# The experts' last 32 slots on 512-column tiles, with their first products ahead of the wide ones

## The chip, the cores and the metric

The kernel runs on one core of a Trainium2 chip. The metric is the device time of one execution in microseconds; lower is better. TensorE does the matrix products, VectorE (DVE in the rows) and ScalarE (ACT) move and transform their results, GpSimd (POOL) issues the indirect DMAs, and SyncE (SP) issues the weight loads. Each engine works off its own instructions in a fixed order, and semaphores hold an instruction back until what it needs is there.

## What is computed

One decoder layer on 2048 tokens of width 1024: a mixer (gated linear attention beside dilated attention), then a mixture of 32 experts, then a last norm. The change lies in the experts. Each token goes to two experts; an expert is a SwiGLU block:

```python
def expert_block(args):
    toks, e = args
    xb = x[toks]
    hb = jax.nn.silu(xb @ w1[e]) * (xb @ w3[e])
    return hb @ w2[e]
y = lax.map(expert_block, (row_tok.reshape(n_blk, MOE_BLOCK), blk_exp))
y = y.reshape(R, D).astype(jnp.float32) * row_w[:, None]
out = jnp.zeros((M, D), jnp.float32).at[row_tok].add(y)
```

w1 and w3 are 1024x512 per expert, w2 is 512x1024, all float32.

## The kernel before

An expert has 160 slots for tokens: a first block of 128 and the **last 32**. The loop over the experts (L1439) is unrolled. For each expert:

- **Weights** (L1292): six parts of 1 MB (half of w1, half of w3, the other halves, two halves of w2) are loaded by SP into `raw`, a pool of six buffers, so one expert's worth. ScalarE rounds each part to `hi` (L1308) and VectorE takes the rest, `lo = raw - hi` (L1308); these two share a pool of five pairs. A buffer of `raw` comes free when it has been split and when the last slots have used it too.
- **First block, first products** (`up`, L1347): 48 wide products of 512 columns, three for each of 8 slices of the 1024 rows and each of w1 and w3 (`nh·hi`, `nl·hi`, `nh·lo`; L1358 to L1360). ScalarE's silu (L1372) and VectorE's product (L1373) make `h`.
- **Last slots, first products** (in `up`, L1367): plain float32 products with 32 columns of weights each. The array is used as four tiles of 32 columns, and the four hold the two halves of w1 and the two halves of w3, 256 columns each: 8 slices x 4 tiles = 32 products. The silu (L1378) and product (L1379) make `hr`.
- **Turning the inner values** (`across`, L1382): four transposes of `h` (L1385) and the split into `hh` and `hl` (L1388); two transposes of `hr` (L1393) and the copy `ht` (L1395).
- **The next expert's inputs** (`turn`, L1330): eight transposes of the gathered rows (L1333), split into `nh` and `nl` (L1336). Every fourth expert, `turn_last` does the same for the last slots of four experts (`nr`).
- **Second products** (`down`, L1398): 24 wide products (L1407 to L1409), scaled out of PSUM by both engines (L1411, L1413) and added to `acc` in DRAM by an indirect DMA (L1415); then 16 products of the last slots on four tiles of 256 columns (L1423), scaled to `yr` (L1426) and added by a second DMA of 128 rows of 1 KB (L1427).

From expert 16 on, a finished block of tokens is taken from `acc`, normed and given out beside each expert (`take`, `scale`, `give`).

The order of each engine's instructions is worked out when the kernel is built: of what a timeline model holds to be ready, the piece that stands first in the program goes first, so a later piece can slip in where an earlier one is not ready. `behind` (L125) forces one instruction after another without a semaphore. A plain float32 product appears as two MATMUL records, one for each pass.

Of the kernel before, what the change touches and what calls it, by code (L numbers as in the profile page):

```python
# [60 lines left out]
class Layer:  # L61
# [1123 lines left out]
    def moe(self):  # L1185
        tc, nc, a = self.tc, self.nc, self.a
        with self.moest as st:
# [9 lines left out]
            acc4 = self.acc.rearrange("t (g c) -> (t g) c", g=4)  # L1197
# [3 lines left out]
            i4A = keep.tile([128, NE], I32, name="i4")  # L1201
# [3 lines left out]
            def entries(es):  # L1205
# [10 lines left out]
                f4 = gp.tile([128, NE], F32, name="f4", bufs=1)  # L1216
                nc.vector.tensor_copy(f4[:, es], irA[:, es, 0])
                nc.vector.tensor_scalar(f4[:, es], f4[:, es], 4.0, self.gcol, OP.mult, OP.add)
                nc.vector.tensor_copy(i4A[:, es], f4[:, es])
# [110 lines left out]
            def turn(G):  # L1330
                tp = tps.tile([128, KD, 128], F32, name="tp")
                for k in range(KD):
                    nc.tensor.transpose(tp[:, k, :], G[:, k * 128:(k + 1) * 128], self.ident)  # L1333
# [13 lines left out]
            def up(w, x, nr=None):  # L1347
# [5 lines left out]
                for half in range(2):  # L1353
                    for m in range(2):
                        raw, hi, lo = w[m][half]
                        for kk in range(4):
                            k = half * 4 + kk
                            nc.tensor.matmul(ps[m], nh[:, k, :], hi[:, kk, :], start=k == 0, stop=False)  # L1358
                            nc.tensor.matmul(ps[m], nl[:, k, :], hi[:, kk, :], start=False, stop=False)  # L1359
                            nc.tensor.matmul(ps[m], nh[:, k, :], lo[:, kk, :], start=False, stop=k == KD - 1)  # L1360
                pr = None
                if nr is not None:
                    pr = rps.tile([128, 256], F32, name="r")
                    for k in range(KD):
                        for g in range(4):
                            raw = w[g // 2][k // 4][0]
                            nc.tensor.matmul(pr[32 * g:32 * g + 32], nr[:, k, :], raw[:, k % 4, (g % 2) * 256:(g % 2) * 256 + 256],  # L1367
                                             start=k == 0, stop=k == KD - 1, skip_group_check=True, tile_position=(0, 32 * g))
# [5 lines left out]
                hr = None  # L1374
                if nr is not None:
                    hr = gp.tile([128, 256], F32, name="hr", bufs=1)
                    by, to = (lambda t: t.rearrange("t (p k) -> t k p", k=2)), hr[64:128].rearrange("t (k p) -> t k p", k=2)
                    nc.scalar.activation(to, by(pr[0:64]), AF.Silu)  # L1378
                    nc.vector.tensor_tensor(to, by(pr[64:128]), to, OP.mult)  # L1379
                return h, hr  # L1380

            def across(h, hr):  # L1382
                tp = mm.tile([128, 4, 128], F32, name="mm")
                for k in range(4):
                    nc.tensor.transpose(tp[:, k, :], h[:, k * 128:(k + 1) * 128], self.ident)  # L1385
# [3 lines left out]
                ht = None  # L1389
                if hr is not None:  # L1390
                    tr = rps.tile([128, 2, 64], F32, name="r")
                    for c in range(2):
                        nc.tensor.transpose(tr[:, c, :], hr[64:128, c * 128:(c + 1) * 128], self.ident[64:128, 64:128])  # L1393
                    ht = gp.tile([128, 2, 2, 32], F32, name="ht", bufs=1)
                    nc.vector.tensor_copy(ht, tr.rearrange("p c (u s) -> p u c s", u=2))  # L1395
                return hh, hl, ht

            def down(w2, x, it, irs, e=None):  # L1398
                hh, hl, ht = x
# [17 lines left out]
                if ht is not None:  # L1417
                    ir, i4 = irs
                    pr = rps.tile([128, 256], F32, name="r")
                    for k in range(4):  # L1420
                        raw = w2[k // 2][0]
                        for g in range(4):
                            nc.tensor.matmul(pr[32 * g:32 * g + 32], ht[:, k // 2, k % 2, :], raw[:, k % 2, g * 256:g * 256 + 256],  # L1423
                                             start=k == 0, stop=k == 3, skip_group_check=True, tile_position=(0, 32 * g))
                    yr = yp.tile([128, 256], F32, name="yr", bufs=1)
                    nc.vector.tensor_scalar(yr, pr, ir[:, 1:2].bitcast(F32), None, OP.mult)  # L1426
                    added(nc.gpsimd.indirect_dma_start(out=acc4, out_offset=bass.IndirectOffsetOnAxis(ap=i4, axis=0),  # L1427
                                                       in_=yr, in_offset=None, compute_op=OP.add), e)
# [10 lines left out]
            for e in range(NE):  # L1439
# [9 lines left out]
                h = across(*up((w1, w3), x, nr[:, :, at:at + 32]))  # L1449
                at += 32  # L1450
                if e + 1 < NE:
                    x = turn(G.pop(e + 1))
                    if e % 4 == 1:
                        nr, at = turn_last(R, 32 * min(4, NE - 1 - e)), 0
                    for t, c in zip(self.turned, self.crossed):
                        self.behind(t, c, "what the tensor engine waits for comes first")
                if e == 0:
                    self.firstst.close()
                    yp = pool("e_y", 1)
                down(w2, h, itA[:, e], (irA[:, e], i4A[:, e:e + 1]), e)  # L1460
# [124 lines left out]
```

## Time and profile before

| what | value |
|---|---|
| three runs | 2205.49, 2211.96, 2216.13 us; median 2211.96 |
| the profiled execution | 2214.42 us; its span 2212.6 us |
| TensorE busy | 2096.8 us, 95% of the span |
| VectorE, ScalarE, GpSimd busy | 57%, 48%, 24% of the span |
| mean granted TensorE clock | 0.972 of full speed |
| the experts' stage | from about 1316 us to about 2178 us of the span |

The busy share of TensorE counts a product from its start to its modelled end, and products overlap; idle time and lost time between products is read from the timeline, by the distance from one start to the next.

### The profile page before, as it was taken

The page shows a single profiled execution, that of the slowest core. Times are in us where ns is not written, and L with a number is a line of the kernel's source. Part 1 is how long each engine was busy: PE and PEld are TensorE (multiplying, and loading weights), DVE is VectorE, ACT ScalarE, POOL GpSimd, SP SyncE. Part 2 cuts the span into 40 slices and gives each one's busy share as a digit, 9 for nine tenths or more (in the row PEclk, how much of TensorE's full clock was granted, in tenths as well). Part 3 has the DMA queues.
Part 4 walks back from the last instruction along what each step waited for, and adds up shares of the span by engine and source line. Part 5 has one row for each costly group of instructions (what it writes and reads, how often), then busy time and mean ns, then how long its engine had stood idle before and what let it go on. Part 6 is the DMA issues. An engine that isn't in the chain of part 4 may idle for free.

```text
span 2212.6 us, 38640 instructions
## 1 busy us (share of the span) xinstructions
PE 2096.8 (95%) x15306; PEld 1571.0 (71%) x15306; DVE 1272.2 (57%) x2469; ACT 1057.2 (48%) x1809; POOL 530.6 (24%) x370
## 2 busy tenths in 40 slices
PE   7999999999997999999999968999999999999993
PEld 7799889799885666666667756666767766666662
DVE  5203346424435556666646775676767677766762
ACT  5412335522323367767723334465555556555651
POOL 2000000000002002441421253632222344424432
PEclk9999999999998999999989969999999999999996
DMA  8333333333325614453358827788878889988973
GB/s 252 109 127 102 115 117 117 98 113 124 96 85 179 192 68 134 150 132 92 96 174 283 253 100 249 253 315 300 291 278 301 310 307 351 329 303 294 319 276 106
DMA packets 189033, 436.59 MB, mean 197 GB/s; under 512 B 35041, under 2 KB 106530, under 8 KB 162978
## 3 DMA queue, kind: packets, MB, share of 16 engines
q1 hardware_dynamic: 139090, 347.65, 44.5%
q0 software_dynamic: 21488, 60.36, 10.3%
q10 hardware_dynamic: 28272, 26.09, 4.0%
q8 instruction: 122, 2.00, 0.4%
q14 instruction: 61, 0.50, 0.1%
HBM read 342.48 MB, written 92.08 MB: 196 GB/s over the span
## 4 chain that ended last, share of the span: by engine, by line
PE 83%; DMA 6%; DVE 4%; issue 2%; POOL 2%; ACT 1%; SPq 0%; ACTq 0%; DVEq 0%; POOLq 0%
PE r L1367 5%; PE s L561 5%; PE mm L1360 5%; PE mm L1358 5%; PE mm L1359 4%; PE mm L216 4%; PE mm L217 4%; PE mm L193 4%; PE mm L218 4%; PE mm L194 4%; PE mm L195 4%; PE po L590 4%; PE pt L575 4%; PE mm L1407 3%; PE mm L1408 3%; PE r L1423 3%
## 5 line engine op out<-in xcount | busy, mean ns | idle before, releaser
L1308 DVE TENSOR_TENSOR lo<-raw,hi 128x2048 fp32r<-128x2048 f32 x192 | 438.3, 2290 | 133.0 <-ACT hi L1308 132.3
L1308 ACT CAST hi<-raw 128x2048 fp32r<-128x2048 f32 x192 | 364.6, 1905 | 191.7 <-DMA raw<-expert_w 170.8
L567 ACT ACTIVATE P<-P,st 128x256 f32<-128x256 f32 (+1 forms) x384 | 173.9, 455 | 96.9 <-DVE st L565 92.6
L216 PE MATMUL mm<-whi,nh 128*128 128x256 f32 x768 | 219.9, 286 | 0.0
L218 PE MATMUL mm<-whi,nl 128*128 128x256 f32 x768 | 218.2, 284 | 0.0
L217 PE MATMUL mm<-wlo,nh 128*128 128x256 f32 x768 | 217.8, 284 | 0.0
L1360 PE MATMUL mm<-lo,nh 128*128 128x512 f32 x512 | 206.6, 405 | 1.1 <-DVE lo L1308 1.1
L1358 PE MATMUL mm<-hi,nh 128*128 128x512 f32 x512 | 205.0, 401 | 1.7 <-ACT nh L1336 1.3
L1359 PE MATMUL mm<-hi,nl 128*128 128x512 f32 x512 | 201.6, 394 | 0.0
L131 POOL TENSOR_TENSOR ss<-ss,mhalf 128x1 f32<-128x1 f32 (+1 forms) x32 | 28.9, 902 | 695.2 <-DVE ss L130 695.1
L565 DVE CUSTOM_DVE_ANT_0 P<-s,amask 128x256 f32<-128x256 f32 (+1 forms) x384 | 124.9, 362 | 66.2 <-PE s L561 42.9
L193 PE MATMUL mm<-nh,whi 128*128 128x512 f32 x384 | 154.5, 402 | 0.0
L194 PE MATMUL mm<-nl,whi 128*128 128x512 f32 x384 | 153.1, 399 | 0.0
L195 PE MATMUL mm<-nh,wlo 128*128 128x512 f32 x384 | 152.7, 398 | 0.0
L1367 PE MATMUL r<-raw,nr 128*32 128x256 f32 x2048 | 148.5, 383 | 0.0
L216 PEld LDWEIGHTS mm<-whi,nh 128*128 128x128 f32 x768 | 145.5, 189 | 2.0 <-issue 0.7
L217 PEld LDWEIGHTS mm<-wlo,nh 128*128 128x128 f32 x768 | 145.6, 190 | 0.8 <-DVE wlo L179 0.4
L218 PEld LDWEIGHTS mm<-whi,nl 128*128 128x128 f32 x768 | 144.9, 189 | 0.1
L1415 POOL DMA_INDIRECT acc<-y,it x32 | 84.6, 2642 | 205.6 <-ACT y L1411 195.8
L561 PE MATMUL s<-k,q 64*128 64x256 f32 (+1 forms) x768 | 132.8, 416 | 0.4 <-DVE st L565 0.3
L1360 PEld LDWEIGHTS mm<-lo,nh 128*128 128x128 f32 x512 | 96.6, 189 | 42.7 <-issue 14.0
L179 DVE TENSOR_TENSOR wlo<-raw,whi 128x1024 fp32r<-128x1024 f32 x48 | 57.0, 1220 | 112.7 <-ACT whi L178 112.7
(345 smaller groups left out, 4252.3 us busy)
## 6 DMA issues: line engine op xcount, KB each, us to landing
raw<-expert_w SPq DMA_DIRECT2D x192, 1024.0 KB, 9.7
raw<-w_in ACTq DMA_DIRECT2D x48, 512.0 KB, 5.0
fb<-fac SPq DMA_DIRECT2D x24, 384.0 KB, 7.5
x<-x SPq DMA_DIRECT2D x16, 512.0 KB, 5.0
og<-og SPq DMA_DIRECT2D x32, 256.0 KB, 3.8
xr<-x SPq DMA_DIRECT2D x32, 256.0 KB, 3.2
v<-av SPq DMA_DIRECT2D x8, 1024.0 KB, 7.2
hp<-xr SPq DMA_DIRECT2D x32, 256.0 KB, 2.3
```

Source lines behind the costliest of these rows:

```text
L193: nc.tensor.matmul(ps, hi[:, k, ms], nh[q][:, k, :], start=k == 0, stop=False)
L194: nc.tensor.matmul(ps, hi[:, k, ms], nl[q][:, k, :], start=False, stop=False)
L195: nc.tensor.matmul(ps, lo[:, k, ms], nh[q][:, k, :], start=False, stop=k == KD - 1)
L216: nc.tensor.matmul(ps[:, j, :], h, hi[:, k, :], start=j == 0 and k == 0, stop=False, skip_group_check=True)
L217: nc.tensor.matmul(ps[:, j, :], h, lo[:, k, :], start=False, stop=False, skip_group_check=True)
L218: nc.tensor.matmul(ps[:, j, :], l, hi[:, k, :], start=False, stop=k == KD - 1, skip_group_check=True)
L561: nc.tensor.matmul(ps[:, h, 0:w], KQ[p, br][hs, 128 * blk:128 * blk + 128], keys(br, blk, KQ[p, "k"][hs]), start=True, stop=True, skip_gro ...
L1308: split = nc.scalar.copy(hi, raw), nc.vector.tensor_tensor(lo, raw, hi.bitcast(F32), OP.subtract)
L1358: nc.tensor.matmul(ps[m], nh[:, k, :], hi[:, kk, :], start=k == 0, stop=False)
L1359: nc.tensor.matmul(ps[m], nl[:, k, :], hi[:, kk, :], start=False, stop=False)
L1360: nc.tensor.matmul(ps[m], nh[:, k, :], lo[:, kk, :], start=False, stop=k == KD - 1)
L1367: nc.tensor.matmul(pr[32 * g:32 * g + 32], nr[:, k, :], raw[:, k % 4, (g % 2) * 256:(g % 2) * 256 + 256], start=k == 0, stop=k == KD - 1, ...
```

## The change

The last slots' work is taken out of `up`, `across` and `down` into functions of its own.

- `up_last`: the four tiles now hold w1 and w3 for an even slice and w1 and w3 for an odd slice, 512 columns each: 4 pairs of slices x 4 tiles = 16 products. The even and the odd sums stand in PSUM rows 0 to 63 and 64 to 127; a copy by ScalarE (64x512) and an addition by VectorE (64x512) join them, then silu (32x512) and two products (32x256 each) make `hr`.
- `down_last`: 8 products of 512 columns instead of 16 of 256; again two sums, joined by a scaled copy on ScalarE (64x512) and a scaled addition on VectorE (64x512); the DMA adds 64 rows of 2 KB instead of 128 rows of 1 KB.
- Order: `up_last` stands ahead of `up`, and each half of the wide products is put behind the last slots' products that read the same half. `down_last` stands ahead of the transposes of `h`, which are put behind its last product; the transposes for the next expert are put behind those. The wide second products come last. In expert 0 the wide first products stand first and the next expert's inputs are turned ahead of the transposes of `h`.

```diff
-            def up(w, x, nr=None):
+            def up_last(w, nr):
+                pr = rps.tile([128, 512], F32, name="r")
+                halves = []
+                for k in range(0, KD, 2):
+                    for g in range(4):
+                        kk, raw = k + g // 2, w[g % 2][k // 4][0]
+                        lasts = nc.tensor.matmul(pr[32 * g:32 * g + 32], nr[:, kk, :], raw[:, kk % 4, :],
+                                                 start=k == 0, stop=k == KD - 2, skip_group_check=True, tile_position=(0, 32 * g))
+                    halves.append(lasts)
...
+                nc.scalar.copy(sm, pr[64:128])
+                nc.vector.tensor_tensor(sm, pr[0:64], sm, OP.add)
+                nc.scalar.activation(sg[32:64], sm[0:32], AF.Silu)
+                by = lambda t, u: t[:, 256 * u:256 * u + 256].rearrange("t (p k) -> t k p", k=2)
+                for u in range(2):
+                    to = hr[64 + 32 * u:96 + 32 * u].rearrange("t (k p) -> t k p", k=2)
+                    nc.vector.tensor_tensor(to, by(sm[32:64], u), by(sg[32:64], u), OP.mult)
+                return hr, halves[1::2]
+            def up(w, x, halves=None):
...
+                            first = nc.tensor.matmul(ps[m], nh[:, k, :], hi[:, kk, :], start=k == 0, stop=False)
+                            if halves and kk == 0:
+                                self.behind(first, halves[half], "the raw weights come free early")
...
+                    self.inner = nc.tensor.transpose(tp[:, k, :], h[:, k * 128:(k + 1) * 128], self.ident)
+                    if after is not None:
+                        self.behind(self.inner, after, "the last slots' products cover the inner values")
...
+            def down_last(w2, hr, ir, i2, e):
+                ht = across_last(hr)
+                pr = rps.tile([128, 512], F32, name="r")
+                for k in range(0, 4, 2):
+                    raw = w2[k // 2][0]
+                    for g in range(4):
+                        kk, f = g // 2, g % 2
+                        last = nc.tensor.matmul(pr[32 * g:32 * g + 32], ht[:, k // 2, kk, :], raw[:, kk, f * 512:f * 512 + 512],
+                                                start=k == 0, stop=k == 2, skip_group_check=True, tile_position=(0, 32 * g))
+                yr = yp.tile([64, 512], F32, name="yr", bufs=1)
+                nc.scalar.activation(yr, pr[64:128], AF.Copy, scale=ir[64:128, 1:2].bitcast(F32))
+                nc.vector.scalar_tensor_tensor(yr, pr[0:64], ir[0:64, 1:2].bitcast(F32), yr, op0=OP.mult, op1=OP.add)
+                added(nc.gpsimd.indirect_dma_start(out=acc2, out_offset=bass.IndirectOffsetOnAxis(ap=i2, axis=0),
+                                                   in_=yr, in_offset=None, compute_op=OP.add), e)
+                return last
...
-                h = across(*up((w1, w3), x, nr[:, :, at:at + 32]))
+                if e == 0:
+                    h = up((w1, w3), x)
+                hr, halves = up_last((w1, w3), nr[:, :, at:at + 32])
+                if e:
+                    h = up((w1, w3), x, halves)
                 at += 32
+                if e == 0:
+                    x = turn(G.pop(1))
...
+                h = across(h, down_last(w2, hr, irA[:, e], i2A[:, e:e + 1], e))
                 if e + 1 < NE:
-                    x = turn(G.pop(e + 1))
+                    if e:
+                        x = turn(G.pop(e + 1), self.inner)
...
-                down(w2, h, itA[:, e], (irA[:, e], i4A[:, e:e + 1]), e)
+                down(w2, h, itA[:, e], e)
```

## Rows read from the trace of the kernel before

**Rows 1.** Stretches of the experts' stage: length, busy by engine, PEclk, DMA share, GB/s

```profile
1630.00:1680.00 50.00, 50.00 (x364) 35.20 (x364) 35.80 (x26) 29.16 (x22) 12.14 (x6) 1.00 0.83 298
2030.00:2080.00 50.00, 48.47 (x330) 33.16 (x329) 35.16 (x28) 30.67 (x25) 22.91 (x12) 1.00 0.97 349
```

**Rows 2.** What TensorE waited for, 1330 to 2180: total us, times, longest

```profile
PE mm L1385 <- DVE h L1373: 11.0, 3, 6.9
PE mm L1407 <- ACT hh L1388: 3.4, 4, 1.6
PE r L1393 <- DVE hr L1379: 2.4, 3, 1.1
```

**Rows 3.** What SP's load queue waited for, 1380 to 2180: total us, times, longest

```profile
SPq L1303 <- PE r L1367: 443.4, 58, 19.5
SPq L1303 <- PE r L1423: 209.5, 58, 15.0
```

**Rows 4.** One stretch of 3 us inside an expert, columns as in rows 1

```profile
1606.00:1609.00 3.00, 3.00 (x48) 1.75 (x50) 2.12 (x2) 0.72 (x1) 0.00 (x0) 1.00 0.00 0
```

**Rows 5.** Timeline, VectorE and ScalarE, one expert: start, length, what, idle before

```profile
1632.63 0.69 DVE L1373 TENSOR_TENSOR h<-mm,h 128x512 f32<-128x512 f32 x1 [2.64 <-PE mm L1360]
1633.24 2.28 DVE L1308 TENSOR_TENSOR lo<-raw,hi 128x2048 fp32r<-128x2048 f32 x1
...
1635.87 0.59 ACT L1388 CAST hh<-mm 128x512 fp32r<-128x512 f32 x1 [0.17 <-PE mm L1385]
1636.48 0.69 DVE L1388 TENSOR_TENSOR hl<-mm,hh 128x512 fp32r<-128x512 f32 x1 [0.32 <-ACT hh L1388]
...
1657.87 0.69 DVE L1373 TENSOR_TENSOR h<-mm,h 128x512 f32<-128x512 f32 x1 [1.55 <-PE mm L1360]
```

**Rows 6.** Timeline, TensorE: the last slots' products of one expert and their neighbours

```profile
1622.41 0.39 PE L1359 MATMUL mm<-hi,nl 128*128 128x512 f32 x1
1622.73 1.05 PE L1367 MATMUL r<-raw,nr 128*32 128x256 f32 x10
1623.71 0.50 PE L1360 MATMUL mm<-lo,nh 128*128 128x512 f32 x1
...
1624.05 0.39 PE L1358 MATMUL mm<-hi,nh 128*128 128x512 f32 x1
1624.28 0.39 PE L1359 MATMUL mm<-hi,nl 128*128 128x512 f32 x1
...
1629.38 0.64 PE L1367 MATMUL r<-raw,nr 128*32 128x256 f32 x8
...
1632.45 2.79 PE L1367 MATMUL r<-raw,nr 128*32 128x256 f32 x46
...
1635.17 0.66 PE L1385 MATMUL mm<-ident,h 128*128 128x128 f32 x4
...
1642.67 1.93 PE L1423 MATMUL r<-raw,ht 128*32 128x256 f32 x32
```

**Rows 7.** Timeline of a late expert: transposes of hr, copy, second products

```profile
1949.39 0.33 PE L1393 MATMUL r<-ident,hr 64*128 64x64 f32 x2
...
1949.76 0.29 DVE L1395 COPY ht<-r 128x128 f32<-128x128 f32 x1 [0.84 <-PE r L1393]
...
1950.15 1.93 PE L1423 MATMUL r<-raw,ht 128*32 128x256 f32 x30 [0.43 <-ACT hh L1388]
...
1952.68 0.41 PE L1367 MATMUL r<-raw,nr 128*32 128x256 f32 x2
```

**Rows 8.** Groups by line, 1580 to 1780: count, busy us, mean ns, idle before

```profile
L1388 DVE TENSOR_TENSOR hl<-mm,hh 128x512 fp32r<-128x512 f32 x8 | 5.5, 691 | 2.6 <-ACT hh L1388 2.6
L1388 ACT CAST hh<-mm 128x512 fp32r<-128x512 f32 x8 | 4.7, 587 | 1.3 <-PE mm L1385 1.3
L1426 DVE TENSOR_SCALAR yr<-r,ir 128x256 f32<-128x256 f32 x8 | 3.8, 476 | 0.0
L1379 DVE TENSOR_TENSOR hr<-r,hr 64x256 f32<-64x256 f32 x8 | 3.4, 428 | 2.5 <-ACT hr L1378 2.4
```

More of the change, by code (lines that the diff above doesn't have):

```diff
@@ L1215, in entries @@
                                           reason="the whole table is read")
[L1216 to L1219, printed above, removed]
+                f2 = gp.tile([64, NE], F32, name="f2", bufs=1)
+                nc.vector.tensor_copy(f2[:, es], irA[0:64, es, 0])
+                nc.vector.tensor_scalar(f2[:, es], f2[:, es], 2.0, self.gcol[0:64], OP.mult, OP.add)
+                nc.vector.tensor_copy(i2A[:, es], f2[:, es])
             places = keep.tile([128, NT], I32, name="places")
@@ L1328, in gather_last, with turn @@
                 return R
-            def turn(G):
+            def turn(G, after=None):
                 tp = tps.tile([128, KD, 128], F32, name="tp")
                 for k in range(KD):
-                    nc.tensor.transpose(tp[:, k, :], G[:, k * 128:(k + 1) * 128], self.ident)
+                    t = nc.tensor.transpose(tp[:, k, :], G[:, k * 128:(k + 1) * 128], self.ident)
+                    if after is not None:
+                        self.behind(t, after, "these cover the copies of the inner values")
                 nh = gp.tile([128, KD, 128], F32R, name="nh")
@@ L1388, in across, with across_last, down @@
                 self.crossed = nc.scalar.copy(hh, tp), nc.vector.tensor_tensor(hl, tp, hh.bitcast(F32), OP.subtract)
[L1389 to L1399, printed above, removed]
+                return hh, hl
+            def across_last(hr):
+                tr = rps.tile([128, 2, 64], F32, name="r")
+                for c in range(2):
+                    nc.tensor.transpose(tr[:, c, :], hr[64:128, c * 128:(c + 1) * 128], self.ident[64:128, 64:128])
+                ht = gp.tile([128, 2, 2, 32], F32, name="ht", bufs=1)
+                nc.vector.tensor_copy(ht, tr.rearrange("p c (u s) -> p u c s", u=2))
+                return ht
+            def down_last(w2, hr, ir, i2, e):
[13 more added lines that the diff above has]
+                return last
+            def down(w2, x, it, e=None):
+                hh, hl = x
                 y = yp.tile([128, D], F32, name="y", bufs=1)
@@ L1416, in down @@
                                                    in_=y, in_offset=None, compute_op=OP.add), e)
[L1417 to L1428, printed above, removed]
             G, R = self.first
@@ L1486, in moe @@
                 x = turn(gx)
-                down(w2, across(*up((w1, w3), x)), it, None)
+                down(w2, across(up((w1, w3), x)), it)
                 m = nc.values_load(cur[:, 2:3], min_val=0, max_val=NT)
```

35 lines of the change are left out of this document (11 added, 24 removed).

## The prediction

> **What bounds the kernel now.** I read the stage of the experts first, in stretches. In the middle of the stage TensorE is busy for 50.00 of 50 us at full clock, while VectorE has 35.80, ScalarE 29.16 and the DMA share is 0.83; late, with the norm's blocks beside the experts, TensorE still has 48.47 of 50 and the DMAs are at 0.97 [rows 1]. So TensorE's own sequence sets the pace; late, the DMAs come near it. Second, what TensorE waited for: over the whole stage only 11.0 us on `h`, in three places, one of 6.9 us in expert 0, and a few us on `hh` and `hr` [rows 2]. Waits are not where the time lies. Third, the load queue: SP waited 443.4 us and 209.5 us for the last slots' products to let go of a buffer of `raw` [rows 3], and the sign of it is a stretch of 3 us per expert in which no DMA byte moves at all [rows 4]. That is slack that the DMAs don't get; but since TensorE isn't starved in that stretch (3.00 of 3.00), it costs no time in the middle of the stage. An expert lasts 25.24 us there, from one `h` to the next [rows 5].
>
> So the question is what the change does to the sequence on TensorE. The fourth view is the timeline of one expert, at the last slots' products [rows 6]. They come in three pieces among the wide first products (10, 8 and 46 records) and one piece of 32 after the wide second products.
>
> - **Price of a column.** 32 records in 1.93 us and 8 in 0.64 us: six more groups of four tiles take 1.29 us, so 0.215 us a group of four passes over 256 columns. The piece of 46 fits (ten more groups than the piece of 8: 2.15 us).
> - **Incomplete groups.** 46 records are 23 products, five full sets of four tiles and one of three: 12 groups. 10 records are 5 products: a set of four and one alone, 4 groups. With 2 groups for the 8, that is 18 where full sets need 16: 2 x 0.215 = 0.43 us an expert lost.
> - **Price of a visit** to the four-tile form. The wide product before the piece of 10 starts at 1622.41, the next at 1623.71; at the usual 0.23 (1624.05 to 1624.28) it would be 1622.64, and the one after it comes 0.34 later instead of 0.23. So the piece takes 1.07 + 0.11 = 1.18 us, of which 4 groups are 0.86: about 0.32 us for going in and out. Four visits: 1.28 us an expert.
>
> **The change part by part.**
>
> *512 instead of 256 columns.* The same columns pass: 16 + 8 groups at 0.215 become 8 + 4 groups of twice the columns, at 0.43 by the same rate. No row shows a 512-column group; by these rows the change is 0, and a fixed part per group would be a gain (rival below).
>
> *First products ahead of the wide ones.* They read `raw` alone, so they need no split, and with their place ahead of the wide ones two pieces remain of three (one for each half, or one for both if the four parts have landed): visits go from 4 to 3, at best 2. Value taken: one visit less, -0.32. Incomplete groups: with the pieces cut at the halves all sets are full, -0.43. Bound on the other side: a set cut open now wastes up to 2 x 0.43 = 0.86, so up to +0.43 against now.
>
> *Buffers free early.* SP's waits [rows 3] move to the start of the expert for w1 and w3, and to its middle for w2. SP has nothing else queued here than loads. Gain in the middle of the stage 0, as TensorE isn't starved; late, where the DMAs stand at 0.97, the idle stretch is the only reserve, and a gain there is possible: 0 taken, -9 us at most (all of TensorE's 1.53 us idle in 50, over some 300 us of late experts).
>
> *`down_last` ahead of the transposes of `h`.* Today the piece of 46 covers `h` (1632.45 to 1635.17, while `h` is done at 1633.32 [rows 5, 6]). Afterwards the transposes of `hr` and the second products, 4 x 0.43 = 1.72 us, cover it: enough for 0.69 us of VectorE. But a new wait is laid open: the second products need `ht`, and `ht` needs the transposes of `hr`. In the program they follow the wide products, and nothing that is allowed stands between: the transposes of `h` and the next expert's are put behind. The nearest row is the same chain in a late expert: transposes 1949.39, copy 1949.76, second products 1950.15 after 0.43 us idle (put down to `hh`, but it is the copy, which ends at 1950.05, that came last) [rows 7]. So +0.43. Below: 0, if the next expert's first products slip in there, as they do at 1952.68 [rows 7]. Above: `h` itself, 0.69 us on VectorE, becomes ready in the same moment and goes first: 1.12.
>
> *`hh` and `hl`.* The eight transposes for the next expert still cover them, as today; `yr` on ScalarE (0.59 by `hh`) now stands just ahead of `hh`. It starts when the last second product ends and is done about when the four transposes (0.66 [rows 6]) are: 0, at most +0.3.
>
> *More work behind PSUM.* VectorE: an addition (0.69 by `hl`), one more product (0.43), a longer `yr` (0.69 for 0.48): +1.33 us an expert [rows 8]. ScalarE: a copy and a scaled copy, +1.2 us by the 0.59 of `hh`, and a longer silu. Today VectorE has 35.80 in 50, that is 18.0 in an expert; 19.4 in 25 is no bound. The part of `up_last` lies beside 11 us of wide products (48 x 0.23), so 0; without that cover it would be the chain of copy, addition, silu and product, about 2.2 us. GpSimd's second add has half the rows, at 24% busy: 0.
>
> *Expert 0, the ends.* In the wait of 6.9 us the next expert's eight transposes (about 1 us) now come, but the second products must be done ahead of the transposes of `h`: 0 taken, +-2. At the end, the add of `y` instead of `yr` is the last: 0.
>
> **Sum.** Per expert -0.32 - 0.43 + 0.43 = -0.32 us; with 31 experts after the first, -10 us. Late experts have more pieces today (the two second products and two first ones of the next expert that slip in at 1952.68 [rows 7]): about two more visits in some ten experts, which the fixed order takes away, 10 x 2 x 0.32 = -6 us. Together -16 us, from the profiled 2214.4 to 2198; the median lies 2.4 us below the profiled execution, so **2196 us**.
>
> **The rivals.**
>
> *Better still.* The wait for `ht` is filled by the next expert's first products, and those come in one piece: -0.43 and -0.32 more, 31 x 0.75 = 23 us: 2173. For it: such fill-ins are in the trace. Against: a product that slips in leaves its set incomplete.
>
> *A fixed part per group.* If a group of four had a fixed part, half as many groups would save it 12 times an expert. Against it: a group takes 0.215 and a plain wide product of as many array columns 0.23 [rows 6], so no fixed part shows; with the difference of 0.015 as its size it is 0.18 us an expert, 6 us: 2190. The Trainium skill (TensorEngine Tiling (Array Packing), Instruction Overhead) states an overhead of some 60 cycles for each matmul; as an estimate from that page, 48 fewer instructions an expert at 25 ns would be 1.2 us, 37 us over the kernel, and the trace of before does not show it.
>
> *No gain: `h` ahead of `ht`.* Both are ready within a few tenths of a microsecond after the wide products, and `h` stands first in the program: the wait is 1.12 instead of 0.43, +0.69 x 31 = 21 us on the forecast: 2217. It decides as soon as the wait isn't filled.
>
> *Slower: a split in the way.* Today `lo` of the next part starts 0.61 us after `h` has begun [rows 5], because `raw` came late [rows 3, 4]. With `raw` there early, the splits are held by the five `hi`/`lo` pairs alone, and then the next expert's second part is split while the wide first products still run: VectorE is in a `lo` of 2.28 us when they end, and `h`, `ht`, the second products and everything behind them on TensorE wait for it. Six of them fill 13.7 of 25.2 us, so a moment picked at random falls into one with a chance of 0.54 and waits 1.14 us: 0.62 an expert, 19 us on top of 2217: 2236. It decides if `lo` starts less than 2.28 us ahead of the end of the wide products; if it does so in every expert the time is past 2250. On this side stands a rule of the Trainium skill as well (TensorEngine Tiling (Array Packing), PSUM Bottleneck): tiles speed up TensorE, not the emptying of PSUM. The change adds to the latter only; the rows show VectorE with room on average, and not when it is asked.
>
> *Slower: more pieces.* Four visits as now, and one open set of 512 columns an expert, 0.86: 0.32 + 0.86 over the forecast is 37 us in the worst case, 2233; with one such set in two experts and four visits, 2219 to 2226.
>
> **How the numbers follow.** A difference of 0.5%, 11 us, is about what a measurement of this kernel can tell from none: below 2201 is faster, above 2223 slower. Chances: the forecast 0.29 (of which 0.04 would be measured as no change), better still 0.13, the fixed part 0.04; `h` first 0.21; a split in the way 0.22; more pieces 0.11. Faster 0.42, no change 0.25, slower 0.33. The likeliest case is the forecast, its own range 2186 to 2206. The range for 8 in 10 takes in most of the better case and of the split in the way: 2172 to 2240.
>
> **What would show it.** In the profile after: the first products' pieces per expert (two, of 16 records each) and no visit inside them; the stretch without DMA gone, and SP's wait for the last slots' products smaller; the idle time of TensorE ahead of the second products at 0.43 or less an expert (at 1 us or more, the `h` or `lo` rival holds, told apart by what VectorE does just then); an expert at about 24.9 us in the middle of the stage. A group of 512 columns at clearly less than 0.43 us speaks for the fixed part. The forecast is wrong if TensorE's waits of the kind in [rows 2] grow from 17 us to over 30.

## The result and the profile after

The changed kernel takes 2288.8 us (median of 2281.52, 2285.16, 2292.43 and 2294.84), the kernel before beside it on the same chip 2212.25 us (2205.49 to 2216.13): a ratio of 1.0348, 95% interval 1.0305 to 1.0391. It is 76.5 us **slower**, where 16 us faster was forecast and 2240 was the upper end of the range. The profiled execution took 2285.16 us, its span 2283.3 us.

TensorE is now busy for 2087.0 us, 91% of the span, against 2096.8 us and 95%. So it has a little less work, as forecast, and stands still far more. The stretches that answer to [rows 1], in the same columns:

```profile
1630.00:1680.00 50.00, 45.72 (x244) 29.64 (x243) 32.39 (x25) 25.67 (x22) 7.90 (x5) 0.97 0.81 291
2030.00:2080.00 50.00, 44.31 (x235) 30.41 (x233) 37.82 (x32) 31.61 (x27) 18.04 (x10) 1.00 0.78 273
```

TensorE loses 4.3 us in the first stretch, where it lost nothing before, and 5.7 us in the second, where it lost 1.5. No other engine took over: VectorE and ScalarE have no more than 38 of 50 us. It is waits, and they answer to [rows 2] (1330 to 2250 us, since the stage now ends later; total us, times, longest):

```profile
PE r L1421 <- ACT hi L1308: 40.2, 16, 4.3
PE r L1357 <- DVE nr L1346: 23.5, 8, 3.0
PE r L1421 <- DVE ht L1411: 23.3, 12, 2.5
PE r L1421 <- issue: 6.9, 4, 2.3
PE r L1409 <- DVE hr L1369: 4.6, 1, 4.6
```

L1421 are the last slots' second products, L1357 their first products. The first, third and fourth line are the same wait, that for the copy `ht`, put down to three releasers; the timeline shows which is right. Here is one expert after, at the end of its wide first products (in the timelines of this document, rows that stand between those shown are left out):

```profile
1603.89 2.29 DVE L1308 TENSOR_TENSOR lo<-raw,hi 128x2048 fp32r<-128x2048 f32 x1 [0.15 <-ACT hi L1308]
1604.43 0.39 PE L1387 MATMUL mm<-lo,nh 128*128 128x512 f32 x1
1604.75 0.34 PE L1409 MATMUL r<-ident,hr 64*128 64x64 f32 x2
1606.11 0.68 DVE L1392 TENSOR_TENSOR h<-mm,h 128x512 f32<-128x512 f32 x1
1606.71 0.28 DVE L1411 COPY ht<-r 128x128 f32<-128x128 f32 x1
1607.04 1.92 PE L1421 MATMUL r<-raw,ht 128*32 128x512 f32 x16 [1.96 <-DVE ht L1411]
```

`hr` is turned at 1604.75 and could be copied at about 1605.1. But VectorE went into `lo`, the split of the next expert's part, at 1603.89 and comes out at 1606.18; then `h`, which also waited, goes first; then the copy, in 0.28 us. The second products start 2.29 us after the first transpose of `hr`. Counted over the whole trace, there are 32 such places, 77.6 us from the start of the second transpose to the products, median 2.43 us. The copy itself takes 0.28 us; with nothing in the way about 0.2 would be left, as an estimate, so some 71 us are lost here. In 30 of the 32 experts a `lo` is running when the wide products end, and `h` starts 1.28 us or more after them; before the change `h` starts within 0.3 us of that end in 22 of 32. All that stands behind on TensorE (the transposes of `h`, those for the next expert, the wide second products) is put behind these products and waits with them.

The second wait comes once in four experts, where the last slots' rows of the next four are turned (`turn_last`):

```profile
1616.36 1.04 PE L1344 MATMUL tp<-ident,R 128*128 128x128 f32 x8
1616.87 2.29 DVE L1308 TENSOR_TENSOR lo<-raw,hi 128x2048 fp32r<-128x2048 f32 x1 [2.12 <-ACT hi L1308]
1619.08 1.22 DVE L1346 COPY nr<-tp 128x1024 f32<-128x1024 f32 x1
1620.35 4.97 PE L1357 MATMUL r<-raw,nr 128*32 128x512 f32 x32 [2.95 <-DVE nr L1346]
```

Before the change the wide first products came next on TensorE and gave `nr` time. Now the first products that read `nr` come next, again with a `lo` ahead of the copy: eight times, 25.6 us from the last transpose's start to the products, some 24 of it lost. And the piece behind the wait takes 4.97 us, where the same 32 records take 3.62 elsewhere. The granted clock tells why (stretches, columns of [rows 1]; PEclk is the third number from the end):

```profile
1619.70:1623.00 3.30, 2.65 (x16) 0.68 (x20) 2.79 (x2) 0.00 (x0) 3.00 (x2) 0.50 0.49 158
1623.10:1626.00 2.90, 2.90 (x27) 1.03 (x18) 0.00 (x0) 0.57 (x1) 0.87 (x1) 1.00 0.63 68
```

TensorE stood still for 2.95 us, and then ran at 1.2 instead of 2.4 GHz for a stretch of 3.4 us. In the stage of the experts there are 15 such stretches (14 of 3.4 us, one of 6.8), 55 us in all, where the kernel before has three of 17 us in all. At half speed the difference is at most (55 − 17) / 2 = 19 us lost.

**The account.** Counted from one expert's transposes of `h` to the next one's, the 31 distances sum to 900.5 us after and 822.7 before: 78 us, so the whole loss lies in this stage. The two waits and the clock lose 71 + 24 + 19 = 114 us; so about 36 us must have been saved beside them. Part of that is idle time which the kernel before had in other places: within these distances TensorE is idle for 96.7 us after and for 15.5 before, so 81 us more in all, and 81 + 19 − 78 = 22 us are left to be saved in its work. The experiments ask for both sides of that.

### The profile page after: what moved, and what is told of

Its sections match the earlier page's. It is cut to its first block, busy times and chain, and to the rows that moved or that the text cites. A ratio compares the mean times of both kernels' runs of the same rounds, so it can differ in the third digit from the quotient of the medians.

```text
span 2283.3 us, 35703 instructions
## 1 busy us (share of the span) xinstructions
PE 2087.0 (91%) x13770; PEld 1525.5 (67%) x13770; DVE 1312.6 (57%) x2533; ACT 1104.8 (48%) x1873; POOL 512.2 (22%) x370
## 5 line engine op out<-in xcount | busy, mean ns | idle before, releaser
L1387 PE MATMUL mm<-lo,nh 128*128 128x512 f32 x512 | 200.0, 391 | 0.0
L1357 PE MATMUL r<-raw,nr 128*32 128x512 f32 x1024 | 151.5, 631 | 24.8 <-DVE nr L1346 23.5
L1447 POOL DMA_INDIRECT acc<-y,it x32 | 101.3, 3166 | 241.8 <-ACT y L1443 239.7
L1421 PE MATMUL r<-raw,ht 128*32 128x512 f32 x512 | 70.0, 667 | 70.4 <-ACT hi L1308 40.2
```

The source lines that it names most:

```text
L1357: lasts = nc.tensor.matmul(pr[32 * g:32 * g + 32], nr[:, kk, :], raw[:, kk % 4, :], start=k == 0, stop=k == KD - 2, skip_group_check=True, ...
```

## The experiments

Two theories for the 76 us. **The order**: what was put between the producers of `ht` and `nr` and their readers went away, and a split stands in the way. **The columns**: the two sums that 512-column tiles leave in PSUM, with a copy and an addition more in each chain, make everything late. Ratios are to the kernel before on the same chip, in brackets the 95% interval.

**Order and columns apart.** `e8_order_only` has the new order with four tiles of 256 columns, as before, so no second sum; `e3_cols_only` has the 512-column tiles in the old order.

```python
# e8: tiles, products, silu and yr of before; up_last, down_last where the change has them
pr = rps.tile([128, 256], F32, name="r")
# e3: the functions of the change, called in the order of before
h = up((w1, w3), x)
hr, _ = up_last((w1, w3), nr[:, :, at:at + 32])
h = across(h)
ht = across_last(hr)
...
down(w2, h, itA[:, e], e)
down_last(w2, ht, irA[:, e], i2A[:, e:e + 1], e)
```

> The new order alone, on tiles of 256 columns as before (32 and 16 products, no sums to join). Theory: the order carries the loss, since the wait for ht and the wait for nr come from it: 2265 to 2295, with gaps ahead of the second products of about 2.4 us. Rival (the wider tiles carry it): 2235 or less.

> The 512-column tiles alone, with their additional additions and copies, in the order of the kernel before: first products behind the wide ones, transposes of hr behind those of h, second products last. Theory: the columns cost nothing (0.43 us for a group of 512 against 2 x 0.215) and the extra work of VectorE and ScalarE is hidden; visits to the four-tile form as before, sets cut open now and then: within 0.5% of the kernel before, 2200 to 2222. Rival: the wider tiles or the doubled work behind PSUM are what costs: 2240 or more.

`e8_order_only`: 2289.38 us, 1.0352 [1.0311, 1.0392], so all of the loss without any of the columns. Its waits (1330 to 2250) are those of the change, and so is its timeline (`lo`, then `h`, then the copy):

```profile
PE r L1412 <- ACT hi L1308: 62.0, 26, 5.2
PE r L1355 <- DVE nr L1346: 23.3, 8, 3.0
```

```profile
1598.31 2.29 DVE L1308 TENSOR_TENSOR lo<-raw,hi 128x2048 fp32r<-128x2048 f32 x1 [0.43 <-ACT hi L1308]
1599.21 0.33 PE L1401 MATMUL r<-ident,hr 64*128 64x64 f32 x2
1600.63 0.69 DVE L1384 TENSOR_TENSOR h<-mm,h 128x512 f32<-128x512 f32 x1
1601.24 0.28 DVE L1403 COPY ht<-r 128x128 f32<-128x128 f32 x1
```

`e3_cols_only`: 2343.39 us, 1.0578 [1.0523, 1.0632], worse than the change itself. I had expected about no change. So the order carries the loss of the change, and yet the columns are not harmless in another order. First the order.

**Taking the wait for `ht` away.** `e1_ht_early` turns and copies `hr` under the wide products: the transposes stand ahead of the last twelve of them.

```diff
+                            if mid and half and m and kk == 0:
+                                ht, turned = mid()
                             first = nc.tensor.matmul(ps[m], nh[:, k, :], hi[:, kk, :], ...)
+                            if mid and half and m and kk == 0:
+                                self.behind(first, turned, ...)
...
-                    h = up((w1, w3), x, halves)
+                    h, ht = up((w1, w3), x, halves, lambda: across_last(hr))
```

> The transposes of hr are put ahead of the last 12 wide first products (experts 1 to 31), so that VectorE copies ht while TensorE still works. Theory: the changed kernel loses its time where the last slots' second products wait for ht, which stands on VectorE behind a lo of the next expert (2.29 us) and behind h (0.69 us): 32 gaps of 2.43 us median, 77.6 us in all, where 0.2 us would do. With ht copied early the gap falls to 0.3 us or less and the time by 55 to 75 us, from 2289 to 2215 to 2235; the wait for h may come back in part, at most 2.0 us less 1.7 us of second products. Rival: the second products wait for something else (the landing of w2, or their PSUM buffer), and VectorE only happens to be busy: the gap stays above 2 us and the time above 2270.

2223.18 us, 1.0053 [1.0036, 1.007]: 2.95% less than the change, 65 us, for the 71 that the trace put down to it. Not all of the 65 is that wait: the half-speed stretches in the stage fall from 55 to 38 us, and TensorE now waits for `hl` instead, 15.6 us. Of the waits the second remains, untouched:

```profile
PE r L1357 <- DVE nr L1346: 23.3, 8, 3.0
PE mm L1443 <- DVE hl L1407: 15.6, 9, 4.9
```

**Which half of it is `lo`?** `e4_lo_held` leaves the order and puts two of the next expert's splits behind the copy of `ht`.

```diff
-                w1, w3, w2 = weights(e, held.get(e, lambda: {})())
+                w1, w3, w2 = weights(e, held.get(e, lambda: {p: [(1, self.copied)] for p in (1, 2)})())
```

> In the changed kernel VectorE's lo of the next expert's second and third part is put behind the copy ht (an order on VectorE alone, no work less). Theory: of the gap of 2.4 us ahead of the second products, about 1.3 us is this lo and about 1.1 us is h (0.69) and ht itself: the gap falls to 1.0 to 1.2 us, 31 times, and the time from 2289 to 2235 to 2255. Rival: the gap is the latency of the chain itself (transposes, h, ht), and the lo fills a time in which VectorE would only wait: less than 15 us gained, 2274 or more.

2255.92 us, 1.0171 [1.0144, 1.0199]. A `lo` is now in the way in one expert instead of 30. The distance falls from 77.6 to 37.0 us in all, median 1.01, and the ratio by 1.77 points, 39 us: the two agree (a new wait for `hl`, 14.2 us, and half-speed stretches of 34 us instead of 55 about balance each other). What is left:

```profile
1600.34 0.34 PE L1409 MATMUL r<-ident,hr 64*128 64x64 f32 x2
1600.52 0.69 DVE L1392 TENSOR_TENSOR h<-mm,h 128x512 f32<-128x512 f32 x1 [1.46 <-PE mm L1387]
1601.12 0.28 DVE L1411 COPY ht<-r 128x128 f32<-128x128 f32 x1
1601.32 2.28 DVE L1308 TENSOR_TENSOR lo<-raw,hi 128x2048 fp32r<-128x2048 f32 x1
1601.46 1.92 PE L1421 MATMUL r<-raw,ht 128*32 128x512 f32 x16 [0.78 <-DVE ht L1411]
```

That is `h` ahead of `ht` alone, 1.12 us from the first transpose to the products. So both rivals on VectorE's order hold at once: of the median 2.43 us, `lo` is 1.4 and `h` with the copy 1.0.

**Filling the wait instead.** `e7_turn_free` lets the next expert's eight transposes slip into it.

```diff
-                        x = turn(G.pop(e + 1), self.inner)
+                        x = turn(G.pop(e + 1))
```

> In the changed kernel the eight transposes for the next expert are no longer put behind the transposes of h. Theory: they slip into the gap ahead of the second products and fill about 0.9 of its 2.4 us; hh and hl then lose their cover (VectorE's 0.69 and ScalarE's 0.59 lie open, or the next expert's first products fill them): 2289 falls by 0 to 27 us, to 2262 to 2289. Rival: TensorE isn't short of work in the gap but held by its place in the queue: no fill, within 6 us of 2289.

2242.24 us, 1.0104 [1.008, 1.0127]: 2.44 points, 54 us, more than the transposes' own time of some 1 us an expert. The waits ahead of the second products fall from 70 to 46 us. Part of the rest is the clock: six half-speed stretches in the stage, 34 us, instead of 15 and 55 us, at most 10 us of time. And the first products of the last slots now come in one piece in all but four experts, where the change has them cut in 23: 68 visits for 91 and 4 open sets for 24, by the prediction's prices some 25 us as an estimate. The price is seen too, the transposes no longer cover `hh`, though it is small:

```profile
PE mm L1439 <- ACT hh L1403: 7.0, 9, 0.8
```

**Taking the wait for `nr` away.** `e2_nr_early` turns the last slots' rows of the next four experts ahead of the wide first products, where these cover the copy.

```diff
+                at += 32
+                if e % 4 == 1 and e + 1 < NE:
+                    nr, at = turn_last(R, 32 * min(4, NE - 1 - e)), 0
                 if e:
                     h = up((w1, w3), x, halves)
-                at += 32
...
-                    if e % 4 == 1:
-                        nr, at = turn_last(R, 32 * min(4, NE - 1 - e)), 0
```

> The transposes for the last slots of four experts (TR, every fourth expert) move from the end of the expert to just behind the last slots' first products, under the wide ones. Theory: at the end they stand directly ahead of the first products that read nr, and TensorE waits about 3.0 us for a copy of 1.22 us that has a lo in front of it, 8 times, 24 us; moved, this goes, and with it most of the 8 half-clock windows of 3.4 us that follow these waits: 2289 falls by 24 to 38 us, to 2251 to 2265. Rival: the wait is shifted to the other side (the transposes now wait for the gathered rows, or the copy holds up VectorE's other work): 2275 or more.

2274.11 us, 1.0285 [1.0244, 1.0326]: 14 us only. The wait for `nr` is gone, but in expert 1 the rows to be turned aren't there yet, and that gives back 13. Nor does the clock gain much: half-speed stretches of 51 us are left of 55.

```profile
PE r L1421 <- DVE ht L1411: 41.3, 21, 2.2
PE r L1421 <- ACT hi L1308: 22.0, 9, 2.5
PE tp L1344 <- DMA R<-n,irg: 13.1, 1, 13.1
```

**Both away.** `e5_ht_nr` is e1's edit and e2's, with expert 1 left where it was.

```diff
+                at += 32
+                if e % 4 == 1 and 1 < e < NE - 1:
+                    nr, at = turn_last(R, 32 * min(4, NE - 1 - e)), 0
...
-                    if e % 4 == 1:
-                        nr, at = turn_last(R, 32 * min(4, NE - 1 - e)), 0
+                    if e == 1:
+                        nr, at = turn_last(R, 128), 0
```

> The early ht of the run with the transposes of hr ahead of the last 12 wide products, together with the early transposes for the last slots of four experts (from expert 5 on; expert 1 keeps its place, where they would wait for the gathered rows). Theory: the two waits are independent, and with both gone few half-clock windows are left: from 2223 by 7 x 3.0 us and some 10 us of clock to 2185 to 2200, faster than the kernel before (2210) by the visits and open sets saved. Rival: what is gained goes into the next wait (hl, or the first products cut into 15 and 1): 2210 or more.

**2181.31 us, 0.9818 [0.9791, 0.9846]**: 1.8% faster than the kernel before and 5.1% than the change, on the change's own tiles and with its order otherwise. Waits (1330 to 2250) and the stretches of [rows 1]:

```profile
PE r L1413 <- DVE hr L1369: 7.8, 2, 5.5
PE mm L1443 <- DVE hl L1407: 5.1, 2, 3.8
PE r L1357 <- DVE nr L1346: 3.0, 1, 3.0
```

```profile
1630.00:1680.00 50.00, 50.00 (x270) 33.10 (x270) 38.49 (x32) 31.94 (x26) 11.07 (x6) 1.00 0.85 302
2030.00:2080.00 50.00, 49.99 (x281) 33.64 (x280) 42.15 (x37) 35.20 (x34) 21.93 (x12) 1.00 0.97 354
```

TensorE is practically never idle in either. The last wait pays twice: from e1 to e5 the ratio falls by 2.35 points, 52 us, where the wait for `nr` falls by 20 us. In e1 every fourth distance is 34.9 us and the one before it 21.4, together 6.5 us over two of 24.9. The 3.0 us of the wait are the largest part; the rest goes with the clock (from 1503 us on e1 has a half-speed stretch every 102 to 106 us, so once in four experts, 3.4 us but for the last; in all 38 us, in e5 17) and with `hl`, for which TensorE waits nine times in e1, 15.6 us, and 5.1 us in e5. The 20 and 10 us of waits and at most 10 of clock make 40 of the 52.

Anything still to be filled? `e11_free_too` adds e7's edit to e5:

```diff
-                        x = turn(G.pop(e + 1), self.inner)
+                        x = turn(G.pop(e + 1))
```

> The version with both waits removed (early ht, early transposes for the last slots; 2181), and the transposes for the next expert no longer behind those of h. Theory: there is no gap left for them to fill, so nothing is gained, and hh and hl lose their cover to the next expert's first products, which now come in two larger pieces: within 15 us of 2181 to either side, 2166 to 2196. Rival: they take the place of the single product that is cut off today (a visit and most of a set of 0.86 us in 19 experts), 2165 or less.

2189.85 us, 0.9837 [0.9813, 0.9862], against e5's 0.9818: no gain. In e5 hardly any idle time is left that something could slip into.

**The columns in the good order.** `e12_order_mended` is e5 with four tiles of 256 columns and no second sum.

```diff
-                pr = rps.tile([128, 512], F32, name="r")
-                for k in range(0, KD, 2):
+                pr = rps.tile([128, 256], F32, name="r")
+                for k in range(KD):
...
-                nc.scalar.copy(sm, pr[64:128])
-                nc.vector.tensor_tensor(sm, pr[0:64], sm, OP.add)
...
+                nc.vector.tensor_scalar(yr, pr, ir[:, 1:2].bitcast(F32), None, OP.mult)
```

> The new order with both waits removed, on tiles of 256 columns with no sums to join. Theory: the columns carry nothing of their own, 24 groups at 0.215 us for 12 at 0.43; what the mended version gains on the kernel before is the order: 2170 to 2195, within 10 us of the version on 512 columns (2181), with smaller losses where a set is cut open. Rival: a fixed part per group or per instruction, which the wider tiles save: 2200 or more, some 20 us and more above the version on 512 columns.

2180.98 us, 0.9802 [0.978, 0.9825], the same as e5. So on the whole the columns bring nothing, and in this order the extra copy and addition cost nothing that shows: the gain is the order's. The two are not alike in every part, though. The order that is built differs (e12 makes 88 visits, e5 54), so the equal times are a balance; that a group of four tiles has no fixed part which 512 columns would halve rests on the pieces themselves, 1.92 us for 16 records of 512 columns and 1.93 for 32 of 256.

**The columns in the old order.** Why, then, is e3 at 2343? Its waits (1330 to 2250), the timeline of one place in it, and a stretch of 500 us in the columns of [rows 1]:

```profile
PE mm L1438 <- ACT hh L1403: 82.5, 29, 6.8
PE mm L1439 <- DVE hl L1403: 40.3, 28, 1.7
```

```profile
1623.73 1.90 ACT L1308 CAST hi<-raw 128x2048 fp32r<-128x2048 f32 x1 [1.81 <-DMA raw<-expert_w]
1625.66 0.58 ACT L1363 COPY sm<-r 64x512 f32<-64x512 f32 x1
1626.27 0.58 ACT L1403 CAST hh<-mm 128x512 fp32r<-128x512 f32 x1
1626.90 0.72 PE L1438 MATMUL mm<-hi,hh 128*128 128x512 f32 x2 [1.85 <-ACT hh L1403]
```

```profile
1500.00:2000.00 500.00, 434.52 (x2176) 285.82 (x2176) 314.09 (x254) 258.42 (x218) 112.06 (x66) 0.90 0.72 250
```

TensorE stands before the wide second products, since `hh` and `hl` stand behind a `hi`, a `lo` and the copy `sm` that joins the sums; the mean granted clock is 0.90 in the stretch, with 29 half-speed stretches, 174 us in all, in the whole stage. Three runs ask what starts it. `e9_cols_join_late` puts the joining copy and addition behind `hh` and `hl`:

```diff
-                nc.scalar.copy(sm, pr[64:128])
-                nc.vector.tensor_tensor(sm, pr[0:64], sm, OP.add)
+                joined = nc.scalar.copy(sm, pr[64:128]), nc.vector.tensor_tensor(sm, pr[0:64], sm, OP.add)
+                for later, earlier in zip(joined, self.crossed):
+                    self.behind(later, earlier, ...)
```

> The 512-column tiles in the order of the kernel before, as in the run with the columns alone (2343), but the copy and the addition that join the two sums stand behind hh and hl on ScalarE and VectorE. Theory: the 133 us that the columns cost in that order come from these two instructions ahead of hh and hl (TensorE's gap between the transposes of h and the wide second products was 3.3 us median, 21 + 11 times), not from the wider tiles: 2205 to 2230. Rival: the wider tiles, or ScalarE's and VectorE's additional work as such, cost the time: 2300 or more.

2349.52 us, 1.0577 [1.0552, 1.0602]: nothing gained, and that theory falls. `hh` now comes ahead of `sm` and is as late, behind `hi`:

```profile
1615.26 1.90 ACT L1308 CAST hi<-raw 128x2048 fp32r<-128x2048 f32 x1 [2.00 <-DMA raw<-expert_w]
1617.07 0.58 ACT L1407 CAST hh<-mm 128x512 fp32r<-128x512 f32 x1
1617.67 0.58 ACT L1366 COPY sm<-r 64x512 f32<-64x512 f32 x1
```

`e10_cols_second_first` puts the next expert's first wide product behind the last slots' second products, which in e3 had slid into its middle and held `raw` (SP waited 529.6 us for them there).

```diff
+                            if self.second and k == 0:
+                                self.behind(first, self.second, ...)
```

> The 512-column tiles in the order of the kernel before, with the second products of the last slots put ahead of the next expert's wide products (in the run with the columns alone they slid into the middle of those, because the joined sums made hr later, and held the raw buffers of w2 until then). Theory: the 133 us of that run come from the late release: raw of w2 comes late, the splits fall on the moment at which hh and hl are wanted; with the release early the time falls to 2215 to 2260. Rival: hh and hl simply have no cover in this order, since the transposes for the next expert no longer stand between the transposes of h and the wide second products; then the gap there stays at 2.5 to 3.5 us and the time at 2320 or more.

2306.37 us, 1.0371 [1.0346, 1.0395]: 2.07 points better than e3, about a third of the loss. The wait for `hh` falls to 22.2 us, and others come: 28.9 us for `h`, and ahead of the second products 23.9 put down to `ht` and 25.0 to `ss`, a tile of the norm on VectorE. Last, `e13_cols_no_join` leaves the joining copy and addition out of both chains, so that the odd slices' sums are missing from `hr` and `yr`; the products are those of e3.

```diff
-                nc.scalar.copy(sm, pr[64:128])
-                nc.vector.tensor_tensor(sm, pr[0:64], sm, OP.add)
...
-                nc.scalar.activation(yr, pr[64:128], AF.Copy, scale=...)
-                nc.vector.scalar_tensor_tensor(yr, pr[0:64], ..., yr, op0=OP.mult, op1=OP.add)
+                nc.vector.tensor_scalar(yr, pr[0:64], ..., None, OP.mult)
```

> The 512-column tiles in the order of the kernel before, with the odd slices' sums left out: neither copy nor addition joins them (for hr and for yr), so the chains behind the products are as short as before, and the products themselves are all there. This part of the computation is left out. Theory: what the columns cost in the order of the kernel before (133 us) is the longer chain from the products to hr and yr, which moves the last slots' second products and with them the loads and splits: without it 2205 to 2235, dearer than the kernel before only by the sets of 512 columns that are cut open. Rival: the 512-column products themselves cost the time in this order: 2290 or more.

2220.13 us, 1.0034 [1.0014, 1.0055]; the waits are small and the clock is back at 1.00:

```profile
PE mm L1434 <- ACT hh L1400: 8.1, 13, 1.0
PE r L1406 <- DVE hr L1366: 7.7, 17, 2.1
```

```profile
1500.00:2000.00 500.00, 489.66 (x2558) 306.82 (x2556) 359.47 (x282) 280.47 (x220) 176.48 (x82) 1.00 0.84 301
```

So in the old order the joining, with the order that is built around it, costs 5.4 points, about 120 us, and the 512-column products nothing that matters. The products are the same but don't stand in the same places: e13 makes 115 visits, e3 70. How the 120 us divide among late releases of `raw`, the cover of `hh` and `hl`, and the clock stays open: each was touched, none apart from the others.

The Trainium skill (TensorEngine Tiling (Array Packing), PSUM Bottleneck) says that tiles speed up TensorE, not the emptying of PSUM. e3 against e13 agrees in that work behind PSUM cost 120 us; but in e3 VectorE and ScalarE are busy for 314.09 and 258.42 of 500 us, so it is the place of that work in their order, and not their pace, that costs. The Trainium skill (TensorEngine Tiling (Array Packing), Instruction Overhead) states some 60 cycles of overhead for each matmul; if they came on top of the columns, half the instructions should have gained (the prediction's estimate was 37 us). The 1.92 and 1.93 us of the pieces and e5 against e12 show nothing of it.

## Why the prediction was wrong

**The step that failed** is the new wait for `ht`, priced at 0.43 us an expert by the one late expert of [rows 7]. It is some 2.2 us in nearly every expert (71 us / 32 places). The prediction named both mechanisms, `h` ahead of `ht` and a `lo` in the way, as rivals, and e4 shows both holding together. What was wrong in them was the word "random": a `lo` at the end of the wide products was priced by chance, at 0.62 us. But the order repeats from expert to expert: a `lo` stands there in 30 of 32, and costs 1.4 us of the median (e4). That it stands there because `raw` is there early is argued; no run holds `raw` back. The rival's own sentence, past 2250 if it is so in every expert, was the right case, and it was left out of the range.

**A step that was missing**: `turn_last`. It stands beside the changed lines and doesn't change itself, but the products that read its `nr` moved from behind 48 wide products to right behind it. That was 24 us, and 52 us with what follows from it (e1 to e5). The prediction asked of `ht` what stands between producer and reader; it should have asked it of every tile that the moved products read.

**Another that was missing**: the granted clock. A wait was priced at its length; here the clock was at half for 3.4 us around or after 15 of some 40 waits of 1.8 to 4.6 us, up to 19 us in all.

**Right**: the price of a group. Sixteen records of 512 columns take 1.92 us, as 32 of 256 did [rows 6], so 0.43 a group of twice the columns, and the columns themselves are worth 0 (e12). The other argument for it, 0.215 us against the 0.23 of a wide product, sets 256 columns beside 512 and shows nothing. Right too that visits would be saved: 91 over the stage for 138, by the prediction's price 47 x 0.32 = 15 us, and 54 in e5.

**Mis-sized**: the open sets. All were to be full, 0.43 us an expert. But the first products come neither in two pieces of 16 records nor away from other products: in nine experts they are one piece of 32, in the others they are cut, mostly into 30 and 2, the last among the wide second products of the expert before or behind them. A set that is cut takes as long as a whole one: pieces of 2, 4 and 6 records take 1.04, 1.05 and 1.06 us, pieces of 30 and 32 take 3.63 and 3.64.

```profile
1643.97 3.63 PE L1357 MATMUL r<-raw,nr 128*32 128x512 f32 x30
1648.19 1.04 PE L1357 MATMUL r<-raw,nr 128*32 128x512 f32 x2
```

Over the trace 24 sets of 512 columns are cut open, 56 of 256 before, and 19 of 512 in e5. At 0.86 and 0.43 us each that is an estimate of 21, 24 and 16 us: the change saves 3 us where 13 were forecast. With the 15 us of visits it makes 18 of the 22 us that were left in the account.

The saving was there under the loss; e5, which takes the two waits away, comes to 0.9818 x 2212 = 2172 us on the kernel before's time, the *better still* rival's 2173. But it doesn't lie where that rival had it, so the agreement is luck. Over the 31 distances e5 saves 34 us: 39.5 in the last 15 (365.1 for 404.7) and 7.5 in the 13 before (325.9 for 333.4), while the first three cost 13 more (97.6 for 84.6). In the middle 24.9 and, every fourth time, 25.8 us stand for 25.24, near the forecast of 24.9.

The counts in the traces say what these are, as an estimate by the prediction's prices. Late, the kernel before makes 67 visits and cuts 31 sets, e5 makes 19 and cuts 4: 15 + 10 = 25 us. TensorE is idle there for 11.4 us before and not at all in e5, and a half-speed stretch of 6.8 us is gone, at most 3.4: together 40 of the 39.5. In the 13 distances before, 29 visits fewer (9 us), sets that cost 3 us more and 0.9 us less of idle time come to the 7.5. In the first three TensorE is idle for 12.8 us instead of 3.2, and at half speed for 10.8 instead of 5.1: 12.5 of the 13, priced at 0 +-2. So the late term, -6 us for two visits in some ten experts, was right in kind and far too small. No run takes these parts away one by one.

**In part**: extra work behind PSUM was costed at nothing under the cover of the wide products. That holds in the new order (e5 against e12) and not in the old (e3 against e13), so it is the order's cover and not the engines' room that makes it free; VectorE is busier in e5 (38.49 of 50 us) than in e3 (314.09 of 500).

By the signs that the prediction set itself: TensorE's waits grew from 17 us to about 100, the mark for wrong was 30; the idle time ahead of the second products is over 1 us, the mark for the `h` or `lo` rival; an expert takes 27 us or more, all but the last, where 24.9 was the sign of the forecast. SP's waits for the last slots' products did move, from 443.4 and 209.5 us [rows 3], but are hardly smaller (1380 to 2250):

```profile
SPq L1303 <- PE r L1421: 329.4, 54, 16.6
SPq L1303 <- PE r L1357: 264.8, 57, 15.1
SPq L1303 <- DVE lo L1308: 153.0, 42, 9.8
```

The load queue now waits far longer for `lo`: 153.0 us, where it was 25.0 before (1380 to 2180). And a stretch almost without DMA work was still there, in the middle of the wait for `ht`, with TensorE idle beside it, where [rows 4] had it busy:

```profile
1604.00:1607.00 3.00, 1.08 (x6) 0.55 (x4) 3.00 (x4) 2.26 (x2) 0.00 (x0) 1.00 0.06 11
```

## What to carry to other kernels

Work that is moved takes its cover with it: for each tile that a moved instruction reads or writes, ask what stood between producer and reader on the waiting engine, and what stands there now. Where the order is fixed when the kernel is built, a long operation in the way (here 2.29 us of `lo` ahead of 0.28 us of copy) tends to be in the way in nearly every round or in hardly any (30 of 32 after, 1 of 32 in e4), so price both cases and not their mean. And when a change loses, look for the gain beneath: here two moves of a few instructions turned 3.5% slower into 1.8% faster.

## What was not expected of the hardware

The clock. In or after single waits of 1.8 to 4.6 us in a TensorE that was otherwise busy, the granted clock fell to half, 15 times in the stage, for 3.4 us and once for 6.8, and the piece of 32 records behind one took 4.97 us instead of 3.62. Not each such wait was followed by one: there are 15 stretches for about 40 places, and the length of the wait doesn't tell which (2.95 us at 1617.4 was, 2.95 at 1734.1 was not). No run here shows what decides it.
